# A hybrid conformer and attention encoder on one core: the tile framework's schedule made with its timeline simulation instead of the default one

## The chip, the core and the metric

The kernel runs on one core of a Trainium2 chip. The time is device microseconds (us) from start to end of one execution; before the change the median of three runs is 2123.19 us (2121.08 to 2124.86). The engines are named as the profile names them: PE (TensorE matmuls), PEld (its weight loads), DVE (VectorE), ACT (ScalarE), POOL (GpSimd), and SP, which here issues DMAs.

## What is computed

One encoder layer is applied to two sequences, a sample of 1024 tokens and a prompt of 512, with model width 2048, and a final RMS norm follows:

```
z = rms_norm(x) @ w_in                                   # 2048 -> 5632, split in seven
conv = conv1d_31(c_val * sigmoid(c_glu))                 # per channel, 31 taps, 1024 channels
conv = silu(layer_norm(conv)) @ w_pw * silu(c_gate)
q, k = rope(q), rope(k)                                  # 8 heads, 2 kv heads, 128 each
attn = banded_softmax_attention(q, k, v, sink) * silu(a_gate)
y    = rms_norm(x + concat(conv, attn) @ w_out)
```

The attention is banded: each block of 128 queries sees its own block of keys and one on either side, and a learned sink takes part in the softmax.

## The kernel before, in words

All matmuls keep single precision accuracy by splitting each operand into a high and a low part. `parts` (L434) does it: ACT copies the high part (L438), DVE subtracts it for the low part (L439). Three matmuls with 512 columns then make one product (high by high, high by low, low by high). A weight chunk is loaded on SP into a `raw` tile and split into an `hl` tile; three of each exist.

PE goes through a list of work items, in this order. First come `Unit`s for the sample (product at L191, a Strassen-like scheme of seven half-sized products, results taken from PSUM by ACT at L217). Then come `Job`s for the prompt (L578): 44 jobs of 48 matmuls each, namely k and v of two groups, eight q, and then eight times a glu, a val, a gate and an attention-gate job. Then the pointwise jobs of the sample's convolution, the output projection as Units again, and the last projection (L1548). Each job has one PSUM bank, taken in turn from the tags `a`, `b`, `a`, `c` (L424). Tag `a` has two banks, `b` and `c` have one each (L422), so a job on `b` can start only when the job four before it has been taken out of its bank. For a glu job that is done by ACT, with a sigmoid into a `g` tile (L843); for gates it is L915.

Beside these, three lanes of background work are spread out between the matmuls by a budget of nanoseconds (`Lane`, `tick`): the attention lane, the lane of the convolution's taps (L906, 29 multiply-adds on DVE for each channel block) and a lane of preparations, among them the layer norm of the sample's convolution (L1309 to L1338). While the prompt's jobs run, the attention lane does the sample's attention, 16 blocks. One block is a chain over four engines:

```
1033  PE   scores s, 3 matmuls for each of 4 heads; two s banks
1036  DVE  scores scaled, masked, with their maximum, into p
1047  ACT  exp with its sum, 4 times;   1044..1052 DVE: tiny tiles
1054  ACT  p scaled by 1/sum, 4 times
1067  PE   transposes of one 128-key chunk into pt, 4 heads; one pt bank
 438  ACT  high part of pt;   439 DVE low part
1062  PE   3 matmuls into pv; then the next chunk (3 chunks, 2 at the ends)
1075  ACT  pv copied out and stored in att_d
```

When all 16 blocks are stored, `attention_sums` (L1155) loads them again, multiplies by the gates (L1167) and makes sums in `g` and `u` tiles (L1148 to L1151).

The order in which the calls are written is not the order on the engines. The framework takes every instruction with its priority and its dependencies, plays the program through against a model of time, and gives to each engine the most urgent instruction that is ready there at that moment. What comes out is one fixed order for each engine, and slots of the tile pools given out along it. On the chip each engine then works through its order, with waits on semaphores between engines.

## Time and profile before

| what | value |
|---|---|
| median of three runs | 2123.19 us |
| the profiled execution | 2123.67 us, its span 2121.9 us |
| PE busy | 2082.3 us, 9330 matmuls |
| DVE busy | 1683.0 us |
| ACT busy | 1100.8 us |
| mean granted PE clock | 0.995 |

The span runs from the first to the last instruction; 1.8 us of the profiled execution lie outside it. PE is busy for nearly all of the span, so what the order of work can change is how long PE stands still, and it stands still for 39.6 us in all. A line of a view that groups instructions gives engine, operation, output and input, the count, busy time and the mean duration of one; a line of the timeline gives start and duration, and in brackets the idle time before and what ended it.

### The profile page before, as it was taken

To read this page: it belongs to the slowest core of one execution; us is meant where nothing else is said; L and a number is where in the kernel's file an instruction comes from. 1 tells how busy PE (TensorE), PEld (TensorE's weight loads), DVE (VectorE), ACT (ScalarE), POOL (GpSimd) and SP (SyncE) were. 2 spreads that over 40 slices of the span, in tenths; PEclk is the share of its full clock that TensorE was granted. 3 is DMA by queue.
4 is the path that set the end of the run, shared out by engine and by line. 5 is a ranking of instruction groups with operands and counts; after the bars stand their busy time and mean duration, and the time that the engine had idled before them with its cause. 6 is when DMAs were issued, how large, how long until landed. Compare 5 with 4: busy or idle time off the path is not lost.

```text
span 2121.9 us, 26800 instructions
## 1 busy us (share of the span) xinstructions
PE 2082.3 (98%) x9330; PEld 1712.7 (81%) x9330; DVE 1683.0 (79%) x2581; ACT 1100.8 (52%) x1796; POOL 104.8 (5%) x124
## 2 busy tenths in 40 slices
PE   8999999999999999899999999999999999998998
PEld 7878888888888888688888888888888888886886
DVE  8658799988898898889887777677898678876543
ACT  6476445333465655555556776345544565643232
POOL 0001110000011111000000000000000002110000
PEclk9999999999999999999999999999999999998999
DMA  8888878764667778854464647987776369798952
GB/s 284 303 285 246 233 177 277 254 202 150 224 186 179 183 166 213 260 177 148 151 217 157 193 158 234 321 297 251 250 242 224 130 221 265 209 266 272 313 170 80
DMA packets 236408, 465.17 MB, mean 219 GB/s; under 512 B 22128, under 2 KB 79856, under 8 KB 236272
## 3 DMA queue, kind: packets, MB, share of 16 engines
q1 hardware_dynamic: 218992, 431.99, 61.3%
q0 software_dynamic: 17280, 31.46, 9.2%
q8 instruction: 73, 1.20, 0.2%
q14 instruction: 63, 0.52, 0.1%
HBM read 319.19 MB, written 144.18 MB: 218 GB/s over the span
## 4 chain that ended last, share of the span: by engine, by line
PE 86%; DMA 5%; DVE 3%; issue 3%; ACT 1%; POOL 0%; SPq 0%; ACTq 0%; POOLq 0%; DVEq 0%
PE a L191 25%; PE c L191 12%; PE a L578 12%; PE c L578 7%; PE b L191 6%; PE b L578 5%; PE s L191 3%; PE s L1033 2%; PE pv L1062 2%; PE a L1548 2%; PE s L1548 2%; DMA a<-ag_d 2%; PE pt L1067 1%; DMA f<-x_s 1%; PE pv L1548 1%
## 5 line engine op out<-in xcount | busy, mean ns | idle before, releaser
L191 PE MATMUL a<-t,hl 128*128 128x512 f32 x2640 | 632.5, 390 | 5.5 <-ACT u L217 3.9
L191 PEld LDWEIGHTS a<-t,hl 128*128 128x128 f32 x2640 | 493.9, 188 | 110.3 <-ACT u L217 6.0
L439 DVE TENSOR_TENSOR hl<-raw,hl 128x1024 fp32r<-128x1024 f32 (+1 forms) x330 | 337.3, 1022 | 187.3 <-ACT hl L438 183.8
L438 ACT ACTIVATE hl<-raw 128x1024 fp32r<-128x1024 f32 (+1 forms) x330 | 296.5, 899 | 346.3 <-DVE raw L138 64.2
L906 DVE SCALAR_TENSOR_TENSOR f<-f,c_w_dw,f 128x1024 f32<-128x1024 f32 (+1 forms) x464 | 454.6, 1009 | 0.5 <-ACT f L901 0.4
L578 PE MATMUL a<-t,hl 128*128 128x512 f32 x1344 | 329.5, 394 | 2.4 <-DVE hl L439 2.3
L191 PE MATMUL c<-t,hl 128*128 128x512 f32 x1320 | 319.2, 389 | 1.9 <-ACT g L217 1.2
L578 PEld LDWEIGHTS a<-t,hl 128*128 128x128 f32 x1344 | 248.6, 188 | 54.0 <-DVE hl L439 3.9
L191 PEld LDWEIGHTS c<-t,hl 128*128 128x128 f32 x1320 | 247.5, 188 | 54.7 <-ACT g L217 2.0
L578 PE MATMUL c<-t,hl 128*128 128x512 f32 x672 | 169.3, 400 | 0.0
L578 PE MATMUL b<-t,hl 128*128 128x512 f32 x672 | 162.3, 392 | 1.5 <-DVE hl L439 1.5
L191 PE MATMUL b<-t,hl 128*128 128x512 f32 x660 | 161.4, 390 | 0.0
L578 PEld LDWEIGHTS b<-t,hl 128*128 128x128 f32 x672 | 125.0, 188 | 27.2 <-DVE hl L439 1.9
L578 PEld LDWEIGHTS c<-t,hl 128*128 128x128 f32 x672 | 126.3, 191 | 25.6 <-DVE hl L439 0.2
L191 PEld LDWEIGHTS b<-t,hl 128*128 128x128 f32 x660 | 123.4, 188 | 25.3
L217 ACT ACTIVATE u<-a 128x512 f32<-128x512 f32 x114 | 67.3, 591 | 75.1 <-PE a L191 64.9
L217 ACT ACTIVATE g<-a 128x512 f32<-128x512 f32 x106 | 62.9, 593 | 81.7 <-PE a L191 71.8
L1548 PE MATMUL a<-hl,t 128*128 128x512 f32 x192 | 74.3, 390 | 0.0
L438 ACT ACTIVATE a<-pt 128x512 fp32r<-128x512 f32 x64 | 38.0, 593 | 53.0 <-PE pt L1067 52.9
L1047 ACT ACTIVATE p<-p,tiny 128x384 f32<-128x384 f32 (+1 forms) x96 | 54.5, 569 | 18.9 <-DVE tiny L1044 14.4
L346 ACT ACTIVATE hl<-raw 128x1024 fp32r<-128x1024 f32 x44 | 46.3, 1052 | 30.7 <-PE a L578 11.2
L1036 DVE CUSTOM_DVE_ANT_0 p<-s,c_mask,c_attn_sink 128x384 f32<-128x384 f32 (+1 forms) x96 | 51.1, 567 | 13.6 <-PE s L1033 13.2
(319 smaller groups left out, 2533.4 us busy)
## 6 DMA issues: line engine op xcount, KB each, us to landing
raw<-w_in SPq DMA_DIRECT2D x171, 512.0 KB, 4.9
raw<-w_out SPq DMA_DIRECT2D x64, 256.0 KB, 4.0
raw<-w_out SPq DMA_DIRECT2D x31, 512.0 KB, 5.4
a<-xT_s SPq DMA_DIRECT2D x50, 256.0 KB, 4.8
raw<-w_pw SPq DMA_DIRECT2D x24, 512.0 KB, 4.9
f<-x_s SPq DMA_DIRECT2D x16, 512.0 KB, 6.8
f<-y_d SPq DMA_DIRECT2D x16, 512.0 KB, 5.8
y_s<-f SPq DMA_DIRECT2D x16, 512.0 KB, 4.4
```

Source lines behind the costliest of these rows:

```text
L191: nc.tensor.matmul(acc, hl[:, l, o, j, :], toks[j][:, r], start=name in FRESH and j == 0 and q == 0, stop=name in LAST and j == HALF - 1 a ...
L217: nc.scalar.activation(t, bank, AF.Copy)
L346: e.nc.scalar.activation(t[:, 0], raw, AF.Copy)
L438: nc.scalar.activation(hi, x, AF.Copy)
L439: nc.vector.tensor_tensor(lo, x, hi.bitcast(F32), ALU.subtract)
L578: nc.tensor.matmul(job.acc[0], hl[:, l, kk // HALF, kk % HALF, :], r, start=i == 0 and p == 0, stop=i == nk - 1 and p == 2,)
L906: nc.vector.scalar_tensor_tensor(t, h[:, j : j + T], w(j), t, ALU.mult, ALU.add)
L1033: nc.tensor.matmul(ps[:, 0:n], qs[:, x, h], k[y][:, keys], start=p == 0, stop=p == 2)
L1036: nc.vector.tensor_tensor_reduce(p[:, 0:n], ps[:, 0:n], mask, SCALE, e.sink[:, g * GROUP + h : g * GROUP + h + 1], ALU.add, ALU.max, accum ...
L1047: nc.scalar.activation(p[:, 0:n], p[:, 0:n], AF.Exp, bias=nm[:, h : h + 1], accum_out=l[:, h : h + 1])
L1062: nc.tensor.matmul(pv, v[x][:, vs], pt[:, y], start=i == 0 and p == 0, stop=i == last and p == 2)
L1548: nc.tensor.matmul(acc, self.mix[self.KS[i]][:, m, b * P : (b + 1) * P], part[l].rearrange("p a b -> p (a b)"), start=i == 0 and p == 0, s ...
```

## The change

One argument is added. The framework then plays the program through its finer timeline simulation when it makes the order; priorities, dependencies, tiles and instructions are the same.

```
-    with tile.TileContext(nc) as tc, ExitStack() as ctx:
+    with tile.TileContext(nc, schedule_with_timeline_sim=True) as tc, ExitStack() as ctx:
         encoder(ctx, tc, a)
```

The instructions of each engine are the same (ACT has one more table load); their order is not. Over the first 40% of PE's order and the last 30%, most rows move by less than 50 places. In between, where the prompt's jobs run, the job matmuls come up to 217 places earlier and the attention's matmuls up to 646 places later. The names below have the tag, a running number and the framework's number.

On PE, a little past the middle of its order, the third and fourth heads of one attention block (`s_1389`, `s_1391`, block with queries `a_1376`) stood between matmuls of a job before:

```order
L1033 MATMUL s_1385_10013<-t1_1251_9218,a_1376_9983 128x384
L578 MATMUL c_1372_9960<-t1_929_7260,hl_1363_9900 128x512 x3
L578 MATMUL c_1372_9960<-t1_933_7288,hl_1361_9852 128x512 x3
L1033 MATMUL s_1389_10031<-t1_1251_9218,a_1376_9983 128x384
L1033 MATMUL s_1389_10031<-t1_1252_9219,a_1376_9983 128x384
L1033 MATMUL s_1389_10031<-t1_1251_9218,a_1376_9983 128x384
L1033 MATMUL s_1391_10037<-t1_1251_9218,a_1376_9983 128x384
L1033 MATMUL s_1391_10037<-t1_1252_9219,a_1376_9983 128x384
L1033 MATMUL s_1391_10037<-t1_1251_9218,a_1376_9983 128x384
L578 MATMUL c_1372_9960<-t1_934_7291,hl_1361_9852 128x512 x3
L578 MATMUL c_1372_9960<-t1_935_7294,hl_1361_9852 128x512 x3
```

They now follow the end of job `a_1624`, thirteen jobs later, and are followed by more of the attention and the layer norm (L609, L650):

```order
L578 MATMUL a_1624_11495<-t1_941_7325,hl_1611_11405 128x512 x3
L578 MATMUL a_1624_11495<-t1_942_7328,hl_1611_11405 128x512 x3
L1033 MATMUL s_1389_10031<-t1_1251_9218,a_1376_9983 128x384
L1033 MATMUL s_1389_10031<-t1_1252_9219,a_1376_9983 128x384
L1033 MATMUL s_1389_10031<-t1_1251_9218,a_1376_9983 128x384
L1033 MATMUL s_1391_10037<-t1_1251_9218,a_1376_9983 128x384
L1033 MATMUL s_1391_10037<-t1_1252_9219,a_1376_9983 128x384
L1033 MATMUL s_1391_10037<-t1_1251_9218,a_1376_9983 128x384
L609 MATMUL s_1393_10043<-ones_274,t1_1294_9472 128x1 x4
L650 MATMUL s_1415_10196<-u_1404_10116,ones_r_276 128x512
L1067 MATMUL pt_1407_10141<-c_ident_930,p_1384_10011 128x128
L650 MATMUL s_1415_10196<-u_1405_10121,ones_r_276 128x512
```

From that `s_1389` on, PE's order has 166 matmuls of attention and layer norm and not one of a job, until the next job, `b_1634`, begins. Before, the place in front of that job held only another job:

```order
L1067 MATMUL pt_1564_11103<-c_ident_930,p_1550_10986 128x128
L1062 MATMUL pv_1561_11076<-a_1565_11108,t1_1253_9220 128x512 x2
L1062 MATMUL pv_1561_11076<-a_1565_11108,t1_1254_9221 128x512
L578 MATMUL b_1634_11581<-t1_918_7218,hl_1628_11536 128x512 x3
L578 MATMUL b_1634_11581<-t1_919_7221,hl_1628_11536 128x512 x3
```

Job `b_1634` needs the one `b` bank, which job `b_1580` held before it; ACT empties it with the sigmoid into `g_1603`. On ACT that row stood before among the high parts of the weights:

```order
L438 ACTIVATE hl_1588_11264<-raw_1577_11183 128x1024
L346 ACTIVATE hl_1600_11323<-raw_1599_11321 128x1024
L843 ACT_TABLE_LOAD
L843 ACTIVATE g_1603_11331<-b_1580_11214 128x512
L438 ACTIVATE hl_1605_11362<-raw_1589_11267 128x1024
L438 ACTIVATE t1_1607_11381<-f_1585_11244 128x512
```

It now stands about 120 rows behind `hl_1605`, after the copies of the last attention block (`a_1565`, `u_1570`), so that emptying the bank comes behind all of them:

```order
L438 ACTIVATE t1_1623_11476<-f_1601_11326 128x512
L438 ACTIVATE a_1565_11108<-pt_1564_11103 128x512
L1075 ACTIVATE u_1570_11138<-pv_1561_11076 128x512
L843 ACT_TABLE_LOAD
L843 ACTIVATE g_1603_11331<-b_1580_11214 128x512
L438 ACTIVATE hl_1642_11628<-raw_1629_11539 128x1024
```

## Prediction

> **What bounds the kernel now.** The page first, for the busy shares; then the waits of PE; then the windows.
>
> ```profile
> span 2121.9 us, 26800 instructions
> PE 2082.3 (98%) x9330; PEld 1712.7 (81%) x9330; DVE 1683.0 (79%) x2581; ACT 1100.8 (52%) x1796; POOL 104.8 (5%) x124
> ```
>
> ```profile
> PE s L650 <- DVE f L645: 7.9, 1, 7.9
> PE a L280 <- ACT t L441: 6.9, 1, 6.9
> PE a L191 <- ACT u L217: 3.9, 4, 1.4
> ```
>
> ```profile
> 350.00:400.00 50.00, 50.00 (x222) 41.36 (x221) 45.22 (x71) 23.49 (x35) 0.00 (x0) 1.00 0.68 230
> 1200.00:1250.00 50.00, 50.00 (x238) 40.56 (x237) 34.12 (x64) 36.89 (x62) 0.00 (x0) 1.00 0.59 193
> 1250.00:1300.00 50.00, 50.00 (x242) 41.62 (x241) 43.54 (x93) 35.55 (x64) 0.00 (x0) 1.00 0.47 147
> ```
>
> PE bounds it. It stands still for 2121.9 - 2082.3 = 39.6 us; 6.9 us are the start, before the first operand is there, and the largest other piece is 7.9 us. In a plain stretch it does 222 matmuls in 50 us, 0.225 us each. In the windows from 1200 to 1300 us, where the prompt's jobs run with the sample's attention, PE is busy for all 50.00 us: the long chain of an attention block costs nothing there because job matmuls fill its waits. So a new order can win at most 39.6 - 6.9 = 32.7 us, and can lose whatever cover it takes away.
>
> **The change: where cover goes.** The order of the changed program (shown above) has one place that is unlike anything before: from `s_1389` on, 166 matmuls of attention and layer norm stand on PE with no job between them. The next job needs bank `b`, and the row that empties it stands on ACT behind the last copy of the last block. PE, ACT and DVE each go through their orders one by one, so this stretch must last as long as the chain of its blocks: the scores of a block stand on PE behind the last transposes of the block ahead, and its queries are split behind that block's last chunk. Before, the same work ran in the shade of jobs. The durations are those of before, grouped from 900 to 1320 us:
>
> ```profile
> L1047 ACT ACTIVATE p<-p,tiny 128x384 f32<-128x384 f32 x48 | 28.9, 605 | 7.7 <-DVE tiny L1045 4.4 <-DVE tiny L1044 3.3
> L438 ACT ACTIVATE a<-pt 128x512 fp32r<-128x512 f32 x44 | 26.1, 594 | 31.7 <-PE pt L1067 31.5
> L1338 ACT ACTIVATE t<-t,c_conv_ln_b,c_conv_ln_g 128x512 f32<-128x512 f32 x16 | 12.3, 808 | 1.4 <-DVE t L1335 1.4
> L1047 ACT ACT_TABLE_LOAD x9 | 11.5, 1283 | 13.8 <-DVE tiny L1045 13.7
> L1048 ACT ACTIVATE tiny<-tiny 128x4 f32<-128x4 f32 x15 | 2.8, 189 | 0.0
> ...
> L901 ACT ACTIVATE f<-f,c_b_dw,c_w_dw 128x512 f32<-128x512 f32 x4 | 3.2, 805 | 0.0
> ```
>
> ```profile
> L906 DVE SCALAR_TENSOR_TENSOR f<-f,c_w_dw,f 128x512 f32<-128x512 f32 x91 | 64.9, 742 | 0.0
> L439 DVE TENSOR_TENSOR a<-pt,a 128x512 fp32r<-128x512 f32 x44 | 30.2, 686 | 13.3 <-ACT a L438 13.1
> L1036 DVE CUSTOM_DVE_ANT_0 p<-s,c_mask,c_attn_sink 128x384 f32<-128x384 f32 x48 | 27.7, 613 | 4.7 <-PE s L1033 4.5
> L1335 DVE TENSOR_TENSOR t<-t,t 128x1024 f32<-128x1024 f32 x8 | 9.8, 1219 | 1.2 <-ACT t L1332 1.2
> L1036 DVE DVE_READ_ACCUMULATOR2_ANT tiny<- 128x1 f32 x60 | 4.9, 82 | 0.0
> L1051 DVE TENSOR_TENSOR tiny<-tiny,tiny 128x4 f32<-128x4 f32 x15 | 2.3, 156 | 4.2 <-ACT tiny L1048 4.2
> ```
>
> Neighbours on one engine overlap by about 0.07 us, so that long rows follow each other at 0.69 us on DVE (L906), 1.15 (L1335), 0.62 (L439). The timeline of one block gives the pieces that go from engine to engine:
>
> ```profile
> 1239.84 2.14 ACT L1054 ACTIVATE p<-p,tiny 128x384 f32<-128x384 f32 x4 [1.65 <-DVE tiny L1052]
> ...
> 1246.44 0.60 ACT L438 ACTIVATE a<-pt 128x512 fp32r<-128x512 f32 x1 [1.12 <-PE pt L1067]
> 1247.07 0.69 DVE L439 TENSOR_TENSOR a<-pt,a 128x512 fp32r<-128x512 f32 x1 [1.97 <-ACT a L438]
> ...
> 1248.38 0.60 PE L1067 MATMUL pt<-c_ident,p 128*128 128x128 f32 x4
> ...
> 1249.02 0.60 ACT L438 ACTIVATE a<-pt 128x512 fp32r<-128x512 f32 x1 [0.54 <-PE pt L1067]
> ...
> 1254.37 1.23 PE L1033 MATMUL s<-t,a 128*128 128x384 f32 x6
> ```
>
> A chunk's period is 1249.02 - 1246.44 = 2.58 us: high part, low part, pv, and the transposes of the next chunk, which wait for the one `pt` bank.
>
> One whole block without cover, from its queries split to those of the next: first score tiles 0.7 (half of 1.23 and a start), then four maxima at 0.613 + 0.082, 2.8; four tiny DVE rows at 0.156, 0.6; four exps at 0.6 and L1048, 2.6; four scalings, 2.1; last transposes 0.4, two periods 5.2, and the third chunk's two halves 1.3; low part of the next queries 0.7. That is **16.4 us**.
>
> The stretch has five blocks, and other rows stand between theirs. I count them in DVE's and ACT's orders and add what doesn't fit into the block's own waits:
> - A, half done when the stretch begins: 14.3 left. The layer norm's square root with two table loads (1.8), a weight's low part (0.7), four L1335 (4.6) ahead of the first low part, of which 4.2 show, and before the second chunk's copy a table load, eight L1338 and L901, L902, of which 5 show: 26.
> - B: 16.4 and six taps (4.1, 0.7 of them hidden): 19.8.
> - C: 16.4, one low part (0.6), three squares on ACT ahead of the scalings (1.9, at the price of L438), and between the chunks twelve taps, four adds and two L1319, 13.1 in all, of which 5.6 fit into the periods: 26.4.
> - D: 16.4, seven taps less 0.7 (4.1), a square root's table load (1.1): 21.6.
> - E, 256 keys and two chunks: 12.4. Again L645, four L1335 and three rows ahead of the first low part (7.3), six rows ahead of the second (2.2), then L1075, a table load and L843 (1.9): 23.8.
>
> Together 118 us. The bound from below is DVE's own work there, whatever the waits: 34 taps, 27 low parts, 18 maxima, 12 adds of 1024 columns and the small rows come to 82 us. PE's work in the stretch is 54 score matmuls at 0.2, 56 transposes at 0.15 (0.60 for 4) and 42 pv at 0.225, 29 us, and 1 for the layer norm: 30. Before, that is all it cost. So PE stands still for 118 - 30 = **88 us** more, and at the least for 82 - 30 = 52.
>
> **The clock.** Two gaps of PE in the timeline show what standing still does to the matmuls behind it:
>
> ```profile
> 878.12 5.97 PE L578 MATMUL a<-t,hl 128*128 128x512 f32 x25 [2.27 <-DVE hl L439]
> ```
>
> ```profile
> 1921.75 1.58 PE L650 MATMUL s<-f,ones_r 128*128 128x512 f32 x2 [7.89 <-DVE f L645]
> 1923.12 1.48 PE L578 MATMUL c<-t,hl 128*128 128x512 f32 x3
> ```
>
> ```profile
> 1900.00:1950.00 50.00, 42.10 (x171) 33.60 (x170) 34.57 (x68) 17.72 (x25) 0.00 (x0) 0.86 0.82 274
> ```
>
> After 2.27 us the next 25 matmuls take 0.24 each, as ever; after 7.89 us the next take 1.48 / 3 = 0.49, and the window's granted clock is 0.86. In a bare block PE rests for about 5 us between its scores and its first transposes, which lies between. If the clock stays halved, PE's steps on the chain (scores 1.2, transposes 3 x 0.6, pv 3 x 0.25: 3.7 a block, 17 in the stretch) about double: +17, and 3 more until it is back. If it does not, 0. I take **+9**. [...]
>
> **Behind the stretch.** The next jobs' weights (`hl_1642`) stand on DVE behind L1167, which needs the last block's output stored and loaded again:
>
> ```profile
> att_d<-u SPq DMA_DIRECT2D x24, 256.0 KB, 3.5
> ...
> a<-att_d SPq DMA_DIRECT2D x8, 512.0 KB, 7.6
> ```
>
> That is 11.1 us from L1075, then some 7 us of DVE rows up to `hl_1642`; job `b_1634` starts 1.5 us after L1075 and covers 48 x 0.225 = 10.8. So 18.1 - 12.3 = **+6**, between 0, if the load goes quicker, and 12.
>
> **What it wins.** L650 of the last part now stands 12 job matmuls of 0.225 later: of its 7.9 us wait that saves **-3**. Elsewhere neighbours change places, a product of one Unit for one of its other bank, and outside the prompt's jobs no weight chunk's place on DVE moves by more than a few tens of rows. ACT's one added table load, 1.283 us, is on an engine that is 52% busy. **0**, with -20 (most of the 32.7 us of waits gone) and +12 (one more bank waited for at each change of stage) as bounds.
>
> **Sum.** 88 + 9 + 6 - 3 = 100 us. The profiled execution's own time is 2123.67 (span 2121.9 and 1.8 around it), 0.5 above the median of the runs shown. 2123.67 + 100 = **2224 us**.
>
> **Rivals.**
> - The bare blocks overlap more than I think, because ACT and DVE take on the next block while one is at its transposes, and only DVE's own 82 us count. Against it: the queries' split stands behind the last chunk in both orders. 2123.7 + 52 + 6 = 2182. Chance 0.13.
> - Worse: each block's rest halves the clock, and PE's 17 us on the chain double all through the stretch: 2123.7 + 88 + 20 + 6 - 3 = 2235. For it speaks the row after 7.89 us, against it that a block's rest is shorter than that. Chance 0.2. [...]
> - Faster: the finer simulation knows this chip's waits better, and the stretch is no stretch. For that, the bank of `b_1580` would have to come free before the attention ends, at row L843 of ACT. It would, only if PE reached `a_1624` so late that the attention's chain had caught up; but its score matmuls stand behind `a_1624` on PE itself. Then the small waits would go, 20 of 32.7 us: 2104. Chance 0.03.
> - No change within 0.2% (about what a measurement of this kernel can tell, 4 us): the gains above and a stretch that costs 20 us only. Nothing in the rows gives that. Chance 0.03.
>
> **How the numbers follow.** The forecast as worked out has 0.61. The range goes from 2182, DVE's bound, to 2250: the halved clock, 2235, and the bound of 12 for other waits. Faster 0.03, same 0.03, slower 0.94.
>
> **What would show it.** The chain of before has `b_1580`, four jobs ahead of `b_1634`, at
>
> ```profile
> 1309.73 10.88 PE b L578 x48
> ```
>
> so that `b_1634` begins at 1309.73 + 4 x 10.88 = 1353, less the 30 us that now come behind. In the profile after, one stretch of some 110 to 130 us, beginning near 1323 us, with PE busy for less than 0.4 of it, a granted clock below 1 there, and the waits "DVE a L439" and "ACT a L438" at PE's pv, "ACT a L438" at its scores, each of several us. DVE is the busiest engine there. After it comes one wait of a job for `hl` of some us. Before and behind it the windows read as they do now. I am wrong if PE's busy time in that stretch is above 0.7, or if the added idle time is spread over the whole span: then the order elsewhere matters, which I put at 0.

## The result, and the profile after

The changed kernel takes 2278.73 us (median of four runs, 2277.63 to 2280.41) where the kernel before, run beside it, takes 2122.7 (median of four): a ratio of 1.0735, with a 95% interval from 1.0722 to 1.0749, or 156 us more. The forecast was 2224 with a range to 2250. Slower was right, and one long stretch is the larger part of it; the size was not.

The page of the changed kernel, the lines that answer to those of before:

```profile
span 2275.8 us, 27001 instructions
PE 2136.1 (94%) x9330; PEld 1735.3 (76%) x9330; DVE 1689.4 (74%) x2581; ACT 1095.9 (48%) x1797; POOL 105.2 (5%) x124
PEclk9999999999999999999999995589999999999999
```

PE stands still for 2275.8 - 2136.1 = 139.7 us, 100 more than before, and its own work takes 53.8 us longer, with the same 9330 matmuls. The dent in the clock says where most of that is. Now the waits of PE:

```profile
PE pt L1067 <- ACT p L1054: 24.2, 6, 7.4
PE pv L1062 <- DVE a L439: 21.0, 15, 5.7
PE pv L1062 <- ACT a L438: 19.2, 24, 2.2
PE a L191 <- ACT u L217: 9.7, 8, 3.9
PE a L191 <- ACT hl L438: 9.1, 3, 4.5
```

The first three are the hand-overs of an attention block; none of them stood among the largest before. The windows show where they lie, in the same columns as those of before (PE, PEld, DVE, ACT, POOL, the clock, DMA):

```profile
950.00:1100.00 150.00, 138.31 (x615) 110.04 (x614) 99.38 (x154) 74.29 (x131) 0.00 (x0) 0.99 0.43 142
1100.00:1350.00 250.00, 250.00 (x1152) 207.53 (x1151) 151.25 (x239) 118.62 (x181) 0.00 (x0) 1.00 0.51 165
1350.00:1550.00 200.00, 124.26 (x419) 87.91 (x418) 118.69 (x225) 87.70 (x156) 0.00 (x0) 0.70 0.50 175
1700.00:1950.00 250.00, 235.10 (x1041) 190.51 (x1040) 186.31 (x321) 122.03 (x232) 9.60 (x11) 0.98 0.62 197
```

The same stretches of the kernel before:

```profile
950.00:1100.00 150.00, 149.84 (x700) 123.01 (x700) 129.48 (x188) 81.54 (x144) 0.00 (x0) 1.00 0.52 165
1100.00:1350.00 250.00, 250.00 (x1171) 205.71 (x1170) 188.57 (x355) 159.28 (x265) 0.00 (x0) 1.00 0.61 199
1350.00:1550.00 200.00, 199.01 (x907) 164.64 (x905) 152.95 (x252) 99.95 (x161) 0.00 (x0) 1.00 0.79 270
```

From 1350 to 1550 us PE stands still for 75.7 us where it stood still for 1.0. The row to learn from is another one, 1100 to 1350. PE is busy for all 250 us in both kernels, so nothing looks wrong; but DVE did 355 rows there and now does 239, and ACT 265 and now 181. Some of the missing rows are the layer norm's (L1335: eight before, none now); the attention's own show in the masked scores, one row for each head, before and after in this window:

```profile
L1036 DVE CUSTOM_DVE_ANT_0 p<-s,c_mask,c_attn_sink 128x384 f32<-128x384 f32 (+1 forms) x32 | 17.3, 577 | 1.9 <-PE s L1033 1.8
L1036 DVE CUSTOM_DVE_ANT_0 p<-s,c_mask,c_attn_sink 128x384 f32<-128x384 f32 (+1 forms) x21 | 11.4, 561 | 15.0 <-PE s L1033 15.0
```

That is eight blocks before and about five after. The attention falls behind in these 250 us, while PE spends its jobs.

The timeline of PE in the stretch has the pieces that the prediction named:

```profile
1354.09 1.23 PE L1033 MATMUL s<-t,a 128*128 128x384 f32 x6
...
1369.35 1.22 PE L1062 MATMUL pv<-a,t 128*128 128x512 f32 x2 [3.79 <-DVE a L439]
...
1393.95 1.99 PE L1067 MATMUL pt<-c_ident,p 128*128 128x128 f32 x4 [7.44 <-ACT p L1054]
...
1477.10 1.22 PE L1062 MATMUL pv<-a,t 128*128 128x512 f32 x2 [5.66 <-DVE a L439]
...
1485.91 13.01 PE L578 MATMUL b<-t,hl 128*128 128x512 f32 x48 [2.60 <-ACT g L843]
...
1518.15 12.09 PE L578 MATMUL c<-t,hl 128*128 128x512 f32 x40 [5.39 <-DVE hl L439]
```

The first bare scores begin at 1354.09, job `b_1634` at 1485.91: 131.8 us. Four transposes take 1.99 us behind this long wait and about 1.05 in most other places of the stretch; four of before took 0.60. The groups of PE from 1354 to 1486 us say how this divides (count, then busy time and mean ns of one, then the idle time before them and who ended it):

```profile
L1062 PE MATMUL pv<-a,t 128*128 128x512 f32 x42 | 27.5, 727 | 31.7 <-DVE a L439 19.4 <-ACT a L438 12.3
L1067 PE MATMUL pt<-c_ident,p 128*128 128x128 f32 x56 | 18.5, 437 | 24.4 <-ACT p L1054 24.1
L1033 PE MATMUL s<-t,a 128*128 128x384 f32 (+1 forms) x54 | 16.2, 436 | 2.9 <-DVE tiny L1036 2.9
```

and the same line of before from 1200 to 1300 us, beside jobs:

```profile
L1062 PE MATMUL pv<-a,t 128*128 128x512 f32 x37 | 12.7, 400 | 0.0
```

About 68 us of the stretch are idle time (59.0 in the three rows, the rest at the layer norm and the next job), and PE's own steps take the other 64, where the prediction counted 30 from the durations at full clock.

### The profile page after: what moved, and what is told of

Its sections match the earlier page's. It is cut to its first block, busy times and chain, and to the rows that moved or that the text cites. A ratio compares the mean times of both kernels' runs of the same rounds, so it can differ in the third digit from the quotient of the medians.

```text
span 2275.8 us, 27001 instructions
## 1 busy us (share of the span) xinstructions
PE 2136.1 (94%) x9330; PEld 1735.3 (76%) x9330; DVE 1689.4 (74%) x2581; ACT 1095.9 (48%) x1797; POOL 105.2 (5%) x124
## 4 chain that ended last, share of the span: by engine, by line
PE 76%; DVE 7%; issue 7%; DMA 4%; ACT 4%; POOL 1%; SPq 0%; POOLq 0%; ACTq 0%; DVEq 0%
PE a L191 19%; PE a L578 13%; PE c L191 10%; PE c L578 6%; PE b L578 6%; PE b L191 5%; DVE f L906 2%; PE s L191 2%; PE pv L1062 2%; PE a L1548 2%; PE s L1548 2%; PE s L1033 2%; PE pt L1067 1%; PE b L1548 1%; PE c L1548 1%
## 5 line engine op out<-in xcount | busy, mean ns | idle before, releaser
L191 PE MATMUL a<-t,hl 128*128 128x512 f32 x2640 | 648.9, 393 | 21.6 <-ACT u L217 9.7
L191 PEld LDWEIGHTS a<-t,hl 128*128 128x128 f32 x2640 | 496.5, 189 | 132.2 <-ACT u L217 13.9
L906 DVE SCALAR_TENSOR_TENSOR f<-f,c_w_dw,f 128x512 f32<-128x512 f32 (+1 forms) x464 | 456.0, 1010 | 0.3
L438 ACT ACTIVATE hl<-raw 128x1024 fp32r<-128x1024 f32 (+1 forms) x330 | 294.2, 897 | 267.6 <-PE c L1548 44.0
L191 PE MATMUL c<-t,hl 128*128 128x512 f32 x1320 | 327.6, 393 | 8.4 <-ACT g L217 3.3
L578 PE MATMUL a<-t,hl 128*128 128x512 f32 x1344 | 322.2, 393 | 3.0 <-DVE hl L439 2.6
L191 PEld LDWEIGHTS c<-t,hl 128*128 128x128 f32 x1320 | 248.3, 189 | 65.1 <-ACT g L217 5.6
L578 PEld LDWEIGHTS a<-t,hl 128*128 128x128 f32 x1344 | 250.2, 188 | 56.8 <-DVE hl L439 3.6
L191 PE MATMUL b<-t,hl 128*128 128x512 f32 x660 | 173.4, 390 | 0.0
L578 PE MATMUL c<-t,hl 128*128 128x512 f32 x672 | 165.4, 398 | 7.0 <-DVE hl L439 5.4
L578 PE MATMUL b<-t,hl 128*128 128x512 f32 x672 | 163.6, 396 | 5.7 <-ACT g L843 2.6
L578 PEld LDWEIGHTS b<-t,hl 128*128 128x128 f32 x672 | 126.4, 190 | 34.1 <-ACT g L843 3.3
L578 PEld LDWEIGHTS c<-t,hl 128*128 128x128 f32 x672 | 126.2, 191 | 34.3 <-DVE hl L439 6.1
L191 PEld LDWEIGHTS b<-t,hl 128*128 128x128 f32 x660 | 123.6, 188 | 25.5
L439 DVE TENSOR_TENSOR a<-pt,a 128x512 fp32r<-128x512 f32 x64 | 44.0, 687 | 74.7 <-ACT a L438 74.6
L438 ACT ACTIVATE a<-pt 128x512 fp32r<-128x512 f32 x64 | 38.1, 595 | 116.5 <-PE pt L1067 116.0
L1062 PE MATMUL pv<-a,t 128*128 128x512 f32 x132 | 59.3, 513 | 36.5 <-DVE a L439 20.1
```

The lines of the kernel that those rows point to most:

```text
L191: nc.tensor.matmul(acc, hl[:, l, o, j, :], toks[j][:, r], start=name in FRESH and j == 0 and q == 0, stop=name in LAST and j == HALF - 1 a ...
L438: nc.scalar.activation(hi, x, AF.Copy)
L439: nc.vector.tensor_tensor(lo, x, hi.bitcast(F32), ALU.subtract)
L578: nc.tensor.matmul(job.acc[0], hl[:, l, kk // HALF, kk % HALF, :], r, start=i == 0 and p == 0, stop=i == nk - 1 and p == 2,)
L906: nc.vector.scalar_tensor_tensor(t, h[:, j : j + T], w(j), t, ALU.mult, ALU.add)
L1062: nc.tensor.matmul(pv, v[x][:, vs], pt[:, y], start=i == 0 and p == 0, stop=i == last and p == 2)
```

## The experiments

Two theories stood at the start. **Bare attention**: what costs is that the attention's matmuls stand on PE without jobs beside them, and the stretch is there because the sigmoid's row of `b_1580` stands behind the attention; take that cause away and the time comes back. **Spread**: the stretch is one place among many, and the order as a whole costs. The first four kernels were to tell them apart. "Finer" is the schedule with the timeline simulation, "default" the other.

### The sums of attention_sums in u tiles (finer)

```
-        s1, s2, s4, s3 = (e.E() for _ in range(4))
+        s1, s2, s4, s3 = (e.U() for _ in range(4))
```

> Schedule with the finer simulation; the four sums of attention_sums go into u tiles, none into g, so that no g tile that needs the finished attention is asked for ahead of the sigmoid's. In PE's order the piece of 166 matmuls without a job is gone; the sample's attention is spread on, with pieces of 66 and 63 later. Theory 'the bare attention is the cost' : the stretch's 102 us above its own 30 go; the two new pieces cost between 0.16 us a matmul (what the pieces of 29 from 950 to 1100 us cost in the changed kernel) and 0.61 (102 / 166), so 21 to 79 us: 2198 to 2256 us. Theory 'the loss is spread over the order, the stretch is one of its places': within 15 us of the changed kernel, 2264 to 2294 us.

Measured: 2306.19 us, ratio 1.0855 (1.0839 to 1.0871). That is 27 us slower than the changed kernel, though the piece of 166 is gone. The waits of PE show what stands in its place:

```profile
PE b L578 <- ACT t L438: 43.9, 2, 43.5
PE pt L1067 <- ACT p L1054: 25.6, 6, 12.0
```

PE waits once for 43.5 us, up to 1601.07. DVE's timeline shows the work that goes on meanwhile, one row of several:

```profile
1574.58 1.22 DVE L1167 TENSOR_TENSOR a<-a,a 128x1024 f32<-128x1024 f32 x1 [8.50 <-DMA a<-ag_d]
```

These are the rows of attention_sums, which take the finished attention times its gates as it is loaded again, and wait for the loads nearly each time. The attention is still late, and PE now waits at the next place behind it: for operands that ACT splits only at 1600.39, after a wait of its own of 32.59 us for the load of the prompt's keys. That this load is late because of attention_sums is argued from the order, not tried. Two bare pieces are there as well: 66 matmuls of the sample's attention from 1461 to 1512 us, and 63 from 1687 to 1725, which are the prompt's and not, as expected, the sample's. The forecast of 2198 to 2256 is missed, and so is the rival's 2264 to 2294. The stall was moved, not removed.

### The sigmoid in a u tile (finer)

```
-        self.sig = e.G()
+        self.sig = e.U()
```

> Schedule with the finer simulation; the glu's sigmoid is written into a u tile in place of a g tile. In PE's order the piece of 166 is cut: from there on eight pieces of 12 to 36 matmuls, about 180 in all, stand at the ends of jobs. Theory 'a long bare chain is what costs, a short piece hides in the bank's slack': 180 x 0.16 = 29 us in place of 102, 2206 us (2195 to 2225). Rival 'the attention costs its own chain wherever no job stands beside it': 180 x 0.61 = 110, 2287 us (2270 to 2300).

Measured: 2279.04 us, ratio 1.0728 (1.0712 to 1.0744): the changed kernel's time, in the rival's range. The windows:

```profile
1100.00:1350.00 250.00, 212.38 (x869) 166.61 (x868) 158.14 (x274) 117.83 (x195) 0.00 (x0) 0.85 0.44 140
1350.00:1550.00 200.00, 166.05 (x707) 132.07 (x706) 118.95 (x200) 93.37 (x149) 0.00 (x0) 0.89 0.61 211
```

The stretch is cut up, as meant, and PE is idle for 37.6 + 34.0 = 71.6 us between 1100 and 1550; in the changed kernel it is 75.7, nearly all in one place. DVE does nearly the same number of rows from 1100 to 1550 in both (274 + 200 here, 239 + 225 there). So my first theory falls in its second half: where the sigmoid's row stands decides where PE waits, not how long.

### The sample's attention left out, default and finer

Each of the sample's 16 blocks copies its queries to its output; everything else stays.

```
+        if self.s == 0:
+            o = e.U([GROUP, P])
+            with e.tc.high_priority(SOON):
+                nc.scalar.activation(o, self.q, AF.Copy)
...
+            return
```

> Leaves out the sample's attention: each of its 16 blocks copies its queries to its output, with the same pauses in the lane; default schedule. It is the base for the next kernel. PE loses 16 blocks, 46 chunks of 4 transposes and 3 products and 138 x 4 score matmuls at 0.15 to 0.225 us, about 270 matmuls of 0.2 and 300 of 0.17: about 100 us less, 2010 to 2040 us on either theory.

> The same left out, schedule with the finer simulation. No stretch can come from the sample's attention. What the finer schedule still costs against the kernel before it is the part that the prediction put at 0. By the marks in the two traces (end of each bank's last matmul), of the 154 us some 15 stand ahead of 950 us and some 24 in the Units after 1700 us, and L650's step gives 13 back: theory 'the order elsewhere costs of its own' +20 to +40 us. Rival 'elsewhere costs nothing, the small losses follow from the attention': within 10 us of the kernel before it.

Measured: 2032.2 us and 2061.83 us (the runs of the second lie between 2057.71 and 2066.85). So about 30 of the 156 us, 29.6 by the medians, are there without the sample's attention, and 126 need it. The 29.6 are in the range that the order elsewhere was given (20 to 40); the prediction had it at 0.

### A new theory: the pace

What both failed edits leave as it is, is how fast the attention moves in PE's order. Count the job matmuls (L578, L191) on PE from the first scores of one of the sample's blocks to those of the next:

```
default:      78  87  90  87  90  87  90 138  78  90  87  93  84  87  90
finer:       180 129  96  96  96 188 216 174 139 141 180  18   0   0   0
```

Under the finer schedule a block uses up about 1.7 times as many jobs (149 on average over its first eleven counts, 87 for most blocks before). After eleven blocks no job is left that may run before the attention's results are needed, and the last blocks are bare. Inside a block, mostly six job matmuls used to stand between the scores of the first two heads and those of the next two; now, where any do, it is mostly 20 to 23. Between a chunk's last transpose and its first product stood 2 to 10; now, in most chunks beside jobs, 22. So each such return to PE costs some 14 job matmuls more (3 us at 0.225), with one engine between (DVE) or two (ACT and DVE). The chip did with less before: the period of a chunk in that trace is 2.58 us, 11 or 12 job matmuls.

If pace is the cause, the default schedule must lose as much when it is given that pace, the finer one must win when a block returns to PE less often, and writing the lane earlier must not help the finer one.

### A slower and a faster lane, in both schedules

```
-RUSH = 1.8
+RUSH = 1.0
```

and 2.5 in the other two. RUSH is the attention lane's rate for the sample, and again later for what is then left of the prompt's attention.

> Default schedule, RUSH 1.0 in place of 1.8, so that the attention lane is written more thinly between the jobs: in PE's order a block of the sample's attention then takes 159 job matmuls from one to the next, where it took 87 and where the finer schedule's takes 140 to 216. The blocks that no longer fit beside the jobs stand in one piece of 198 attention matmuls much later. Theory 'pace': what costs is that a block takes more jobs than there are, whichever schedule makes it so; 198 x 0.61 us = 121, 2243 us (2215 to 2270). Rival 'the finer order as such': the default order stays within 20 us of the kernel before, 2105 to 2145.

> The same RUSH 1.0 with the finer simulation: pieces of 80 and 224. Theory 'pace': 304 x 0.61 = 185, and 30 for the order elsewhere: 2338 us (2290 to 2365). Rival 'the time does not follow the bare matmuls': as the changed kernel, 2265 to 2285.

> Default schedule, RUSH 2.5: a block takes 65 job matmuls, nothing is bare. Theory 'pace': the cover sufficed already, so nothing is won: 2110 to 2135 us. Rival 'a slower attention costs at every pace': 2080 to 2105.

> The finer simulation, RUSH 2.5: the lane is written sooner, but PE's order still has 96 to 212 job matmuls to a block, and pieces of 52, 22, 55, 29 and 162. Theory 'pace, set by the simulated hand-overs and not by where the calls are written': nothing is won; 162 x 0.61 = 99, 107 x 0.4 = 43, the rest 10, 30 elsewhere: 2305 us (2270 to 2325). Rival 'the written order sets the pace': the stretch goes, 2150 to 2200.

Measured: late_default 2279.93 us (ratio 1.0737, 1.0719 to 1.0756), late_finer 2332.7 (1.0996, 1.0973 to 1.1018), early_default 2139.65 (1.0078, 1.0062 to 1.0093), early_finer 2282.84 (1.0747, 1.0725 to 1.0769). The two finer ones lie in their ranges, the two default ones above theirs.

The default schedule, slowed to 159 job matmuls a block, takes what the changed kernel takes. That the two times agree so well is luck, since the 157 us are made up in another way. Its waits:

```profile
PE a L578 <- DVE f L848: 62.2, 1, 62.2
PE pt L1067 <- ACT p L1054: 29.3, 10, 6.0
```

and two of its windows:

```profile
1550.00:1700.00 150.00, 125.43 (x522) 100.40 (x523) 125.08 (x190) 56.70 (x87) 0.00 (x0) 0.90 0.67 230
1700.00:1950.00 250.00, 203.10 (x765) 151.41 (x764) 128.44 (x253) 119.88 (x246) 11.31 (x13) 0.78 0.45 137
```

and, from the timeline, that one job and a row of DVE in its wait:

```profile
1568.51 7.90 PE L578 MATMUL a<-t,hl 128*128 128x512 f32 x24 [62.24 <-DVE f L848]
```

```profile
1515.63 1.23 DVE L1167 TENSOR_TENSOR a<-a,a 128x1024 f32<-128x1024 f32 x1 [7.01 <-DMA a<-ag_d]
```

The job waits for 62.2 us, for a bank that DVE empties behind the rows of attention_sums (by L1379; the waits name L848, a row just behind it that ended last). The sample's attention has no bare piece of a dozen matmuls or more here; that it is late shows in this one wait. The bare piece of 198 matmuls, from 1755 to 1875 us, is the prompt's attention, whose keys are in `f` tiles where the sample's are in `t` tiles:

```profile
1768.24 1.32 PE L1033 MATMUL s<-f,a 128*128 128x384 f32 x6 [0.24 <-DVE tiny L1036]
```

The lane comes to it late: its first scores stand at 1731 us, before at 1420. The piece lasts 119.8 us and costs about 83, an estimate: less some 37 for its own matmuls at 0.15 to 0.225. The forecast had put 121 on this piece and nothing on the wait, so it missed with both. What the run shows is that a lane which uses up more jobs than there are costs time in the default order too, first at the sums that need it and then in the next sequence's attention.

early_finer, with the lane's rate 1.4 times as high, gains nothing, and its longest piece is still 162: writing the lane more densely does not quicken it there (writing it more thinly, late_finer, does slow it). early_default was to be "nothing won"; it is 17 us slower. A denser attention has a price of its own: 10 us of PE's idle time in this window of early_default, where the kernel before has none:

```profile
1100.00:1350.00 250.00, 239.96 (x1093) 194.82 (x1092) 186.45 (x338) 147.16 (x236) 0.00 (x0) 0.97 0.66 223
```

### Fewer returns to PE

The scores of heads 3 and 4 take the `pt` and `pv` banks, which are free then, and the transposes of two chunks out of three an `s` bank, so that they need not wait for the one `pt`.

```
-            ps = e.PS("s", [3 * P])
+            ps = e.PS(("s", "s", "pt", "pv")[h], [3 * P])
...
-            tp = e.PS("pt", [GROUP, P])
+            tp = e.PS("pt" if i == 1 else "s", [GROUP, P])
```

> The finer simulation, with fewer hand-overs of a block between PE and the other engines: the scores of heads 3 and 4 go into the pt and pv banks in place of waiting for the two s banks, and the transposes of the first and third chunk go into an s bank, those of the second into pt. In PE's order a block then takes 83 to 130 job matmuls (one 170) where it took 96 to 216, and the piece of 166 is one of 53. Theory 'pace': 53 x 0.61 to 0.79 (late_default's 157 / 198) = 32 to 42, and 30 elsewhere: 2190 us (2165 to 2215). Rival 'number of hand-overs and pace don't matter': 2260 or more.

> The finer simulation, the transposes alone moved so (first and third chunk into an s bank). The piece is one of 88, five short ones of 20 or less more. Theory 'pace': 88 x 0.61 to 0.79 = 54 to 70, and 30 elsewhere: 2215 us (2190 to 2240), between the changed kernel and the one above. Rival: 2260 or more.

> As the first of these, and the glu's sigmoid in a u tile. A block takes 74 to 140 job matmuls, and no piece is longer than 23, all of them at the ends of jobs, most of them 12 score matmuls that wait for nothing. Theory 'pace': only the order elsewhere is left, 30 us, and what the short pieces take, 0 to 10: 2157 us (2140 to 2175). Rival 'sigmoid in u was no gain before (2279), so it is none here': as the first, 2190 or more.

> The same banks with the default schedule: a block takes 78 to 90 job matmuls as before, nothing is bare. Theory 'pace': the cover sufficed, nothing to win: 2113 to 2133 us. Rival 'fewer hand-overs are worth something on the chip itself': below 2110.

Job matmuls from block to block with both lines:

```
finer, banks: 125 104 130 120 103 125 170 125  95 101  98  88  99  87  83
```

Measured: banks_finer 2163.19 us (ratio 1.0186, 1.016 to 1.0212), transposes_finer 2183.34 (1.0283, 1.026 to 1.0306), banks_sigmoid_finer 2168.28 (1.0211, 1.019 to 1.0233), banks_default 2123.36 (0.9992, 0.998 to 1.0004).

Two lines that change no amount of work take 115.5 of the 156 us away, in the finer schedule alone; in the default one, where nothing was bare, they are worth nothing. What they spare is returns, not distance: 20 to 38 job matmuls still stand between most chunks' transposes and products, but the next chunk's transposes no longer stand behind those products. The windows of banks_finer:

```profile
950.00:1100.00 150.00, 150.00 (x706) 126.22 (x705) 118.07 (x174) 78.33 (x131) 0.00 (x0) 1.00 0.50 162
1100.00:1350.00 250.00, 249.15 (x1169) 208.70 (x1168) 172.90 (x314) 145.85 (x248) 0.00 (x0) 1.00 0.56 180
1350.00:1550.00 200.00, 170.31 (x732) 138.62 (x731) 150.91 (x261) 93.56 (x157) 0.00 (x0) 0.90 0.71 247
1700.00:1950.00 250.00, 247.72 (x1114) 204.16 (x1113) 199.04 (x319) 145.71 (x253) 27.88 (x32) 1.00 0.76 218
```

DVE gets 314 rows done from 1100 to 1350 in place of 239, and PE's idle time from 1350 to 1550 is 29.7 us. That the new banks make the bare chain itself quicker is not the larger part of it: the piece of 166 matmuls, with 65.6 us of PE's idle time in it, is one of 53 with 16.3. Both finer kernels without the sigmoid's edit came out some 30 us below their expectation, just under their ranges: I had added 30 for the order elsewhere, but the edit quickens the prompt's attention too, and in banks_finer PE is idle for 2.3 us from 1700 to 1950, not 14.9, and for 0.0 from 950 to 1100, not 11.7. The other two lie in the ranges of the pace theory. The sigmoid in a u tile wins nothing here either (5 us slower), though no piece is longer than 23: in that kernel PE's longest waits in total are for the sigmoid's own row (11.9 us in four waits of jobs on `b`). No version beats the kernel before; banks_default equals it.

### Both attentions left out

The same edit for both sequences, to find where the 29.6 us lie.

> Leaves out both sequences' attention (each block copies its queries to its output); default schedule. Base for the next kernel: the prompt's 8 blocks are about 240 matmuls of 0.15 to 0.225 us, 45 us less than without the sample's alone, 1975 to 2000 us.

> The same left out, finer simulation; in PE's order nothing is bare in either. Theory 'the 30 us without the sample's attention lie in the neighbours' places around the Units (weights' sums and halves on DVE and ACT behind rows that wait)': 20 to 30 us above the kernel before it. Rival 'they lie with the prompt's attention, whose blocks take more job matmuls than the cover there': within 10 us of it.

Measured: 1993.08 and 1997.02 us. The difference falls from 29.6 to 3.9 us, in the rival's range, so most of the 29.6 needs the prompt's attention. One place shows in the windows of the pair before, default and then finer:

```profile
1550.00:1700.00 150.00, 149.90 (x683) 122.91 (x682) 111.22 (x189) 86.01 (x160) 11.34 (x13) 1.00 0.65 200
1550.00:1700.00 150.00, 139.40 (x603) 111.13 (x602) 96.82 (x169) 75.34 (x144) 3.49 (x4) 0.95 0.50 164
```

In the finer one a piece of 35 matmuls of the prompt's attention stands bare from 1644 to 1661 us. But my theory (the Units' own order) falls only by the net sum. Compared job matmul by job matmul, the finer kernel of either pair is 17 to 18 us behind at about 935 us, where the sample's first Units are done. Without the sample's attention this grows to 34 by the end of the prompt's; without both it shrinks to 13. Some 13 us come back at L650 in both. So the order of the Units up to there does cost about 17 us, and the 3.9 hide it. The first waits of PE without both are

```profile
PE s L650 <- DVE f L645: 7.6, 1, 7.6
PE a L280 <- ACT t L441: 6.5, 1, 6.5
PE a L191 <- ACT u L217: 2.7, 3, 1.4
```

in the default schedule, and in the finer one

```profile
PE a L280 <- ACT t L441: 6.4, 1, 6.4
PE a L191 <- ACT u L217: 6.1, 5, 4.0
PE a L191 <- ACT hl L438: 3.5, 2, 2.7
```

The finer schedule does remove the wait at L650, and gives it back in small waits of the Units for ACT. One of these in the changed kernel, 3.46 us at 428 us, stands behind a background row on DVE (L835) that waits 2.02 us for its load with a weight's sum (L138) queued behind it.

## Why the prediction was right and wrong

**Right: what bounds, and that the stretch is the largest piece.** There is one stretch of 131.8 us (110 to 130 forecast), with a clock of 0.55 to 0.64 in its windows and the two named waits at `pv`. Its cost, 131.8 - 30 = 102, stands against 88 + 9 = 97. Three signs missed: PE is busy for 0.48 of it and not below 0.4; its longest wait in total, 24.1 us for the scaled scores (L1054), was not named; and none of its scores waits for "ACT a L438".

**That total hides two errors.** The forecast had PE standing still for 88 us and at work for 30 + 9 = 39. It was 68 and 64. The clock term, +9, was mis-sized: PE's steps took 34 us more than the 30 counted, at a granted clock of 0.59 over the whole stretch, and the rival in which each rest halves the clock all through the stretch, with +20, was nearer in this point. The 3 us in that +20 until the clock is back were an estimate; in the kernel before, behind the wait of 7.89 us, the clock read 0.50 from 1921 to 1931 us and 0.97 from 1931 to 1933. How much shorter the stretch would be at full clock isn't shown, since some of the 34 would turn into waiting; no kernel tried it. One reading in the block sums was a little off: the long rows of L906 follow each other every 0.66 us, not 0.69, which makes under 2 us on 34 taps.

**Behind the stretch, +6:** the waits for `hl` came, 2.20 and 5.39 us, at the two jobs behind `b_1634`. By the ends of the jobs in the two traces this made about 10. **L650, -3:** the whole wait of 7.9 us is gone and the slow matmuls behind it (three in 1.48 us before); the end of that bank's work moves by about -13 between the traces, so this gain was mis-sized too.

**The step that failed: "Elsewhere ... 0, with -20 ... and +12 ... as bounds".** 156 - 102 - 10 + 13 = 57 us lie elsewhere, far outside those bounds. About 31 of them are ahead of the stretch (why it began at 1354 and not near 1323): some 14 by 850 us, from small waits of the Units (PE is idle for 18.2 us up to there and not 11.6) and the slower matmuls behind them (ten in 4.02 us at 428 us), and most of the others in short bare pieces from 950 to 1100 us, where PE is idle for 11.7 us and not 0.2. About 22 are behind it, beside the prompt's attention. I looked for one long run without a job, counted it, and took short ones and the distances between rows for harmless. The pair without the sample's attention puts this at 29.6 us net of L650's gain, the pair without both at 3.9.

**The cause, too, was one step short.** The prediction put the stretch down to the bank that is emptied behind the attention. That row decides only where PE stops. Moving it (sums_in_u, sigmoid_in_u) won nothing, or lost 27 us; what pays is the pace: a slower lane in the default order costs 157 us (2279.93 - 2122.86), though at other places than in the finer one, and blocks that use up fewer jobs win 115.5 in the finer order. Why the finer simulation puts some 14 job matmuls more between one of PE's steps in a block and the next was not tried on the chip, and stays open.

**The rivals.** DVE as the bound (2182) is out: DVE is busy for 118.69 of the 200 us from 1350 to 1550. Faster and no change are out. The rival of the halved clock came nearest in the stretch and is still 44 us short in all, mostly because it too had nothing elsewhere.

## What to carry to other kernels

When a scheduler makes the order, count how much of the covering work each step of a long chain uses up, over the whole order, and compare it with what the chain takes on the chip; the bare stretch at the end is only where the account is settled. A busy bottleneck engine hides this: look for the other engines doing less in a window in which it is busy throughout. To mend it, take returns to the busy engine out of the chain; moving the row at which it stops moves the wait.

## What the chip showed beside this

PE stayed slow through most of the stretch, though most of its rests were short: in the timeline from 1354 to 1486 us they run from 0.2 to 7.4 us, all but four below 4, PE was busy for about half the time, and the granted clock was

```profile
1350.00:1400.00 50.00, 24.53 (x79) 15.78 (x77) 28.25 (x65) 27.33 (x50) 0.00 (x0) 0.64 0.43 142
1400.00:1450.00 50.00, 25.36 (x69) 15.92 (x69) 33.64 (x68) 22.64 (x51) 0.00 (x0) 0.60 0.12 37
```

on average over 100 us. A product into `pv` took 727 ns on average, where beside jobs it took 400. Before, behind a single rest of 2.27 us the next 25 matmuls took 5.97 us, 0.24 each. At the start of the stretch stand two rests hardly longer, 2.63 and 2.39 us, with one matmul of 0.50 us between them; the granted clock was 1.00 from 1358 to 1360 us, 0.54 from 1360 to 1362 and 0.50 from 1362 to 1366 (the last line):

```profile
1359.20 0.50 PE L650 MATMUL s<-u,ones_r 128*128 128x512 f32 x1 [2.63 <-DVE u L645]
1362.09 0.47 PE L1067 MATMUL pt<-c_ident,p 128*128 128x128 f32 x1 [2.39 <-ACT p L1054]
1362.34 0.80 PE L650 MATMUL s<-u,ones_r 128*128 128x512 f32 x1
1362.00:1366.00 4.00, 2.76 (x6) 1.27 (x6) 2.22 (x4) 3.90 (x7) 0.00 (x0) 0.50 0.02 4
```

Which of the later rests kept it low, the many short ones or the four between 5.6 and 7.4 us, isn't shown. The matmuls behind a single rest of 3.46 us, the one at 428 us, were slow only briefly: two matmuls took 0.82 us, the next ten 4.02, and the ten after those 2.45, and the granted clock was 0.56 from 430 to 432 us and 1.00 from 432 to 434.
